# Shift and scale of the last four row steps on VectorE, two stages merged, and part of the weight splitting on GpSimd

## The chip, the cores and the metric

The kernel runs on one core of a Trainium2 chip. The metric is the device time of one execution, in microseconds (us); lower is better.

## The reference, cut to what matters

One layer of a diffusion trunk: a first feed-forward half step, a mixer (attention and spatial gating), a second feed-forward half step. Each is modulated by nine vectors that come out of one product with `w_ada`. 128 context and 256 latent tokens, D = 2048, float32.

```python
def adaln(cvec, w_ada, b_ada):
    m = jax.nn.silu(cvec) @ w_ada + b_ada
    return jnp.split(m, N_MOD, axis=-1)

def swiglu_sublayer(x, g, w_gate, w_up, w_down, shift, scale, gate):
    h = rms_norm(x, g) * (1 + scale) + shift
    f = (jax.nn.silu(h @ w_gate) * (h @ w_up)) @ w_down
    return x + 0.5 * gate * f
...
        x_ctx = swiglu_sublayer(x_ctx, ffn1_norm[l], ffn1_w_gate[l], ffn1_w_up[l], ffn1_w_down[l],
                                m_ctx[0], m_ctx[1], m_ctx[2])
```

The change concerns `m[0]` (shift) and `m[1]` (scale) of the first half step, which the first products need.

## The kernel before

All products run in three passes of matmuls: a weight piece is split into a rounded upper part `whi` (ScalarE, L250) and a lower part `wlo` (VectorE, L251), the activations into `hh` and `hl`; `three` (L282 to L284) multiplies lower by upper, upper by lower, upper by upper. Work goes in half steps of 24 matmuls, called slots here: `half()` hands out one split weight half, runs what was set for this slot with `later`, and counts the slot up; `ahead()` splits weights up to four halves ahead. Weights come in chunks of two halves through SyncE's queue into three raw buffers (`pump`, L200).

The first quarter of gate and up (six groups `g`, four PSUM banks each, `first_quarter_staged`) runs in stages over the 16 row steps `k` of D, so that it can begin before all of shift and scale is known: `BLOCKS` gives the steps of a stage. At the end of a stage VectorE adds each bank to a partial sum in SBUF (`part_gh`, `part_gl`, L724). The banks come from a pool of five (`acc`); from the slot of `switch` on, the fourth bank of a group comes from another pool (`mp`). Steps below the last stage are multiplied by unnormalised rows (`make_raw`, L502 and L507); for the last stage the rows are normalised (`make_h`: L527 on VectorE, L537 on ScalarE, L541 on VectorE), and the partial sums are scaled by GpSimd (L726) and shifted by ScalarE (L730).

Shift and scale come from chunks of `w_ada` that TensorE multiplies (`ada_chunk`, L345), one behind each of the first 28 slots, loaded by GpSimd's queue into two buffers (`rawa`). When a unit of steps is complete, `settle` runs `ada_unit`: selection matmuls (L364), bias (L369), scale (L388), then the rows. The other seven vectors are computed later on VectorE from transposed tiles: `ada_tile` (L436) multiplies a tile of `w_ada` with the broadcast vectors `csb`, silu already applied (L405), and sums along the row.

The squares for the norm run at slots 9, 12, 16 and 22 (ScalarE L447 and L452, VectorE L455), the norm at slot 24. Each engine runs its instructions in the order in which the program is written.

Of the kernel before, what the change touches and what calls it, by code (L numbers as in the profile page):

```python
# [35 lines left out]
G0 = QUARTERS[0]  # L36
SEGS = ((0, TC), (TC, T))
TS = T + 2
BLOCKS = ((0, 2), (2, 4), (4, 6), (6, 8), (8, 12), (12, 16))
NPE = 0  # L40
ADA_UNITS = tuple(((0, k0, k1), (1, k0, k1)) for k0, k1 in BLOCKS) + ((tuple((2, k, k + 4) for k in range(0, NPE, 4)),) if NPE else ())
ADA_AFTER = (1,) * (28 + NPE)
NSEL = 4


# [69 lines left out]
class Kernel:  # L115
# [4 lines left out]
    def setup(self):  # L120
        tc, nc, ctx, a = self.tc, self.nc, self.ctx, self.a
        self.main = ctx.enter_context(tc.tile_pool(name="main", bufs=1))
        self.rot = ctx.enter_context(tc.tile_pool(name="rot", bufs=2))
        self.wp = ctx.enter_context(tc.tile_pool(name="wp", bufs=NWP))
        self.acc = ctx.enter_context(tc.tile_pool(name="acc", bufs=5, space=bass.MemoryType.PSUM))
        self.mp = ctx.enter_context(tc.tile_pool(name="mp", bufs=3, space=bass.MemoryType.PSUM))
        self.dram = ctx.enter_context(tc.tile_pool(name="spill", bufs=1, space=bass.MemoryType.DRAM))

        self.par = self.tile1([P, NPAR], "par")
        self.ones = self.tile1([P, P], "ones")  # L130
        nc.vector.memset(self.ones, 1.0 / 1024.0)
# [17 lines left out]
        self.freed = {"W": 0, "A": 0}  # L149
        self.next_split = 0  # L150
# [32 lines left out]
    def pump(self):  # L183

        nc = self.nc
        room = {"W": self.room, "A": NADA}
        while True:
            can = [self.order[k][n] for k, n in self.issued.items()
                   if n < min(len(self.order[k]), self.freed[k] + room[k])]
            if not can:  # L190
                return
            c = min(can)
            k = self.kinds[c]
            if k == "A":
                raw = self.start.tile([P, CK * CW], F32, tag="rawa", name="rawa", bufs=NADA)
                src = self.a["wada_s"][self.issued[k]]
            else:
                raw = self.wp.tile([P, CK * CW], F32, tag="raw", name="raw", bufs=NRAW)
# [3 lines left out]
            self.issued[k] += 1  # L202

    def first_loads(self):

# [7 lines left out]
        for c in order:  # L213
            k = self.kinds[c]
            i = self.issued[k]
            if k == "A" and i < NADA:
                raw = self.start.tile([P, cols], F32, tag="rawa", name="rawa", bufs=NADA)
            else:
                raw = self.wp.tile([P, cols], F32, tag="raw", name="raw", bufs=NRAW)
# [17 lines left out]
        self.freed["W"] = NADA - na  # L237

    def ahead(self, n=NWP):

        nc = self.nc
        while len(self.split) < n and self.next_split < len(self.pieces):
            c, half = self.pieces[self.next_split]
            if half is not None:
                if c not in self.raw:
                    break
                src = self.raw[c][:, half * 1024:(half + 1) * 1024]
                hi = self.wp.tile([P, 1024], F32R, tag="whi", name="whi")
# [12 lines left out]

    def half(self):
# [131 lines left out]
    def csb_load(self, kh, slot):  # L394
# [309 lines left out]
    def first_quarter_staged(self):  # L704
# [38 lines left out]
        for st, (k0, k1) in enumerate(BLOCKS):  # L743
            for pairs in stage_halves(st):
# [4 lines left out]
                if slot == 0:  # L749
# [374 lines left out]
    def run(self):  # L1124
# [15 lines left out]
        with ExitStack() as st:  # L1140
# [30 lines left out]
            one = [(2, k) for k in range(NPE, KT)] + [(j, k) for j in (3, 4) for k in range(KT)]  # L1171
# [84 lines left out]
def layout(i):  # L1256
# [75 lines left out]
    for qt in range(2):  # L1332
        for kr in range(4):
# [38 lines left out]
```

## Time and profile before

| | |
|---|---|
| median of 3 runs | 2826.48 us (2826.29 to 2827.67) |
| the profiled execution, its own time | 2826.2 us |
| its span | 2824.1 us |
| TensorE matmuls busy | 2797.0 us, 99% |
| VectorE, ScalarE, GpSimd busy | 65%, 36%, 7% |
| DMA | 524.89 MB, mean 186 GB/s |

The span is what the profiler saw from first to last instruction; the time holds what lies around it as well. Shares are means over the span: the first 220 us, where shift and scale are made, differ from the rest.

### The profile page before, as it was taken

The page shows a single profiled execution, that of the slowest core. Times are in us where ns is not written, and L with a number is a line of the kernel's source. Part 1 is how long each engine was busy: PE and PEld are TensorE (multiplying, and loading weights), DVE is VectorE, ACT ScalarE, POOL GpSimd, SP SyncE. Part 2 cuts the span into 40 slices and gives each one's busy share as a digit, 9 for nine tenths or more (in the row PEclk, how much of TensorE's full clock was granted, in tenths as well). Part 3 has the DMA queues.
Part 4 walks back from the last instruction along what each step waited for, and adds up shares of the span by engine and source line. Part 5 has one row for each costly group of instructions (what it writes and reads, how often), then busy time and mean ns, then how long its engine had stood idle before and what let it go on. Part 6 is the DMA issues. An engine that isn't in the chain of part 4 may idle for free.

```text
span 2824.1 us, 39182 instructions
## 1 busy us (share of the span) xinstructions
PE 2797.0 (99%) x15984; PEld 2711.1 (96%) x15984; DVE 1841.8 (65%) x2887; ACT 1015.3 (36%) x1454; POOL 187.4 (7%) x302
## 2 busy tenths in 40 slices
PE   8999999999999999999999999999999999999997
PEld 6889999999999999988888999999999999999997
DVE  4767889798999798765566877554444543333335
ACT  3345432322322244543344445333333223322342
POOL 0031011011111010000000000000000000000000
PEclk9999999999999999999999999999999999999999
DMA  8854676666667675454333653444444433333432
GB/s 349 311 190 166 219 251 240 237 239 241 250 241 253 246 257 197 147 170 141 125 120 116 256 222 137 149 159 162 165 155 151 163 127 129 125 121 138 157 132 80
DMA packets 100035, 524.89 MB, mean 186 GB/s; under 512 B 11024, under 2 KB 18832, under 8 KB 55056
## 3 DMA queue, kind: packets, MB, share of 16 engines
q1 hardware_dynamic: 62224, 371.39, 36.0%
q0 software_dynamic: 37632, 151.01, 15.6%
q8 instruction: 125, 2.05, 0.3%
q14 instruction: 54, 0.44, 0.0%
HBM read 511.88 MB, written 10.49 MB: 185 GB/s over the span
## 4 chain that ended last, share of the span: by engine, by line
PE 99%; DVE 0%; DMA 0%; SPq 0%; ACT 0%; issue 0%; DVEq 0%
PE acc L282 24%; PE acc L284 24%; PE acc L283 24%; PE mp L282 7%; PE mp L284 7%; PE mp L283 6%; PE acc L307 2%; PE acc L308 2%; PE acc L309 2%; PE mp L345 1%; PE mp L858 0%; PE mp L908 0%; PE mp L938 0%; DMA raw<-wada_s 0%; DVE x L1240 0%; PE acc L756 0%
## 5 line engine op out<-in xcount | busy, mean ns | idle before, releaser
L251 DVE TENSOR_TENSOR wlo<-raw,whi 128x1024 fp32r<-128x1024 f32 x640 | 784.5, 1227 | 808.5 <-ACT whi L250 808.1
L250 ACT CAST whi<-raw 128x1024 fp32r<-128x1024 f32 x640 | 670.6, 1050 | 1425.0 <-PE mp L284 1149.9
L282 PE MATMUL acc<-hh,wlo 128*128 128x384 f32 (+1 forms) x2744 | 933.5, 340 | 0.0
L284 PE MATMUL acc<-hh,whi 128*128 128x384 f32 (+1 forms) x2744 | 927.6, 338 | 0.0
L283 PE MATMUL acc<-hl,whi 128*128 128x384 f32 (+1 forms) x2744 | 925.6, 337 | 0.0
L282 PEld LDWEIGHTS acc<-hh,wlo 128*128 128x128 f32 x2744 | 516.6, 188 | 25.5 <-issue 11.3
L283 PEld LDWEIGHTS acc<-hl,whi 128*128 128x128 f32 x2744 | 518.0, 189 | 0.8
L284 PEld LDWEIGHTS acc<-hh,whi 128*128 128x128 f32 x2744 | 516.6, 188 | 0.0
L282 PE MATMUL acc<-gh,wlo 128*128 128x384 f32 x1056 | 357.6, 339 | 0.0
L283 PE MATMUL acc<-gl,whi 128*128 128x384 f32 x1056 | 354.3, 336 | 0.0
L284 PE MATMUL acc<-gh,whi 128*128 128x384 f32 x1056 | 352.8, 334 | 0.0
L436 DVE CUSTOM_DVE_ANT_0 scr<-adaw,csb,par 128x1024 bf16<-128x1024 f32 x224 | 287.3, 1282 | 4.4
L436 DVE CUSTOM_DVE_ANT_0 scr<-adaw,csb,m 128x1024 bf16<-128x1024 f32 x224 | 287.3, 1282 | 4.2
L284 PE MATMUL mp<-hh,whi 128*128 128x384 f32 (+1 forms) x704 | 237.8, 338 | 0.0
L282 PE MATMUL mp<-hh,wlo 128*128 128x384 f32 (+1 forms) x704 | 237.2, 337 | 0.0
L283 PE MATMUL mp<-hl,whi 128*128 128x384 f32 (+1 forms) x704 | 237.0, 337 | 0.0
L421 POOL DMA_DIRECT2D adaw<-wada_t x224 | 118.5, 529 | 1447.9 <-DVE m L436 1352.8
L284 PEld LDWEIGHTS acc<-gh,whi 128*128 128x128 f32 x1056 | 198.5, 188 | 0.0
L283 PEld LDWEIGHTS acc<-gl,whi 128*128 128x128 f32 x1056 | 198.3, 188 | 0.0
L282 PEld LDWEIGHTS acc<-gh,wlo 128*128 128x128 f32 x1056 | 198.0, 188 | 0.0
L283 PEld LDWEIGHTS mp<-hl,whi 128*128 128x128 f32 x704 | 132.7, 189 | 0.0
L282 PEld LDWEIGHTS mp<-hh,wlo 128*128 128x128 f32 x704 | 132.5, 188 | 0.0
(170 smaller groups left out, 2238.5 us busy)
## 6 DMA issues: line engine op xcount, KB each, us to landing
raw<-ws SPq DMA_DIRECT2D x319, 1024.0 KB, 4.9
adaw<-wada_t POOLq DMA_DIRECT2D x224, 512.0 KB, 4.0
rawa<-wada_s POOLq DMA_DIRECT2D x26, 1024.0 KB, 5.9
csb<-crow POOLq DMA_DIRECT2D x6, 1024.0 KB, 7.9
keep<-x SPq DMA_DIRECT2D x8, 768.0 KB, 6.8
rawa<-wada_s SPq DMA_DIRECT2D x4, 1024.0 KB, 8.7
bias<-bias SPq DMA_DIRECT2D x16, 256.0 KB, 4.9
xo<-xT SPq DMA_DIRECT2D x16, 192.0 KB, 5.5
```

The source lines that it names most:

```text
L250: nc.scalar.copy(hi, src)
L251: nc.vector.tensor_sub(lo, src, hi.bitcast(F32))
L282: nc.tensor.matmul(o, lhsT=wl, rhs=xh, start=first, stop=False)
L283: nc.tensor.matmul(o, lhsT=wh, rhs=xl, start=False, stop=False)
L284: nc.tensor.matmul(o, lhsT=wh, rhs=xh, start=False, stop=last)
L307: nc.tensor.matmul(o, lhsT=xh, rhs=wl, start=first and kk == 0, stop=False)
L308: nc.tensor.matmul(o, lhsT=xl, rhs=wh, start=False, stop=False)
L309: nc.tensor.matmul(o, lhsT=xh, rhs=wh, start=False, stop=last and kk == 1)
L345: nc.tensor.matmul(self.ada_bank[r:r + 32, :cols], lhsT=self.csil[:, nsub * kc + q, w0:w0 + 32], rhs=raw[:, q * cols:(q + 1) * cols], star ...
L421: self.nc.gpsimd.dma_start(out=t, in_=self.a["wada_t"][j - 2, kt, kh])
L436: nc.vector.tensor_tensor_reduce(out=scr, in0=t, in1=self.csb[:, v, :], scale=1.0, scalar=init, op0=ALU.mult, op1=ALU.add, accum_out=acc)
```

## The change

Stages three and four (steps 4 to 6 and 6 to 8) become one; `w_ada` chunks on TensorE cover steps 0 to 11 only and end with slot 19. Steps 12 to 15 of shift and scale are made by `early()`: sixteen tiles of 128 x 1024 (two quantities, four steps, two halves of D), each reduced twice on VectorE (once for each vector) at the slots listed in `EARLY`. The vectors' halves are loaded at slots 8 and 19 into one of the three raw buffers, so weights have two until slot 34; their silu runs in four pieces on ScalarE in the two slots behind. From slot 8 to 33 lower parts of odd piece numbers are subtracted on GpSimd. `settle` runs in the middle of a slot too.

```diff
-BLOCKS = ((0, 2), (2, 4), (4, 6), (6, 8), (8, 12), (12, 16))
+BLOCKS = ((0, 2), (2, 4), (4, 8), (8, 12), (12, 16))
+UNITS = ((0, 2), (2, 4), (4, 6), (6, 8), (8, 12))
+EK = 12
-ADA_AFTER = (1,) * (28 + NPE)
+ADA_AFTER = (1,) * 20
+EARLY_CSB = (8, 19)
+EARLY = (11, 12, 13, 14, 15, 16, 17, 18, 22, 23, 24, 25, 26, 28, 30, 32)
+EARLY_END = 34
...
-                nc.vector.tensor_sub(lo, src, hi.bitcast(F32))
+                eng = nc.gpsimd if 8 <= self.slot < EARLY_END and self.next_split % 2 else nc.vector
+                eng.tensor_tensor(out=lo, in0=src, in1=hi.bitcast(F32), op=ALU.subtract)
...
+    def early(self):
...
+        def load(i):
+            if i < len(seq):
+                j, k, kh = seq[i]
+                nc.gpsimd.dma_start(out=tiles[i % 2], in_=self.a["wada_e"][j, k - EK, kh])
+
+        def vectors(kh):
+            if kh == 0:
+                self.ecsb = self.raw_buf("csb")
+                load(0)
+                load(1)
+            src = self.a["crow"]
+            nc.gpsimd.dma_start(out=self.ecsb.rearrange("p (a b) -> p a b", a=2),
...
+        def tile_of(i):
+            j, k, kh = seq[i]
+            for v in range(2):
...
+                nc.vector.tensor_tensor_reduce(out=scr, in0=tiles[i % 2], in1=self.ecsb[:, 1024 * v:1024 * (v + 1)],
+                                               scale=1.0, scalar=init, op0=ALU.mult, op1=ALU.add, accum_out=acc)
+            load(i + 2)
+
+        def end():
+            self.free.append(self.buf.pop("csb"))
+            self.room = NRAW
+            self.scales(0, C_G1, EK, KT)
+            self.make_h_later(self.rs, EK, EK + 1)
+            self.later(self.slot + 1, lambda: self.make_h(self.rs, EK + 2, EK + 3))
...
-                for kk, u in order:
+                for at, (kk, u) in enumerate(order):
+                    if at == 4:
+                        self.settle()
...
-            self.later(8, lambda: setattr(self, "room", NRAW))
+            self.early()
...
-            self.later(31 + NPE, switch)
+            self.later(36, switch)
...
-    nc = _bacc.Bacc("TRN2", target_bir_lowering=False, num_devices=1)
+    nc = _bacc.Bacc("TRN2", target_bir_lowering=False, num_devices=1, dynamic_dma_scratch_size=4096)
```

ScalarE around slots 9 and 10, before (casts L250, squares L452 and L447):

```order
L250 CAST whi<-raw 128x1024
L452 ACTIVATE ssq<-x 128x384
L447 ACTIVATE sq<-x 128x384 x3
L250 CAST whi<-raw 128x1024 x3
L447 ACTIVATE sq<-x 128x384 x4
```

and now (L262 is the cast, L456 the silu of the vectors, which lie in a `raw` buffer, L524 and L519 the squares):

```order
L262 CAST whi<-raw 128x1024
L456 ACTIVATE raw<-raw 128x512 x2
L524 ACTIVATE ssq<-x 128x384
L519 ACTIVATE sq<-x 128x384 x3
L262 CAST whi<-raw 128x1024
L456 ACTIVATE raw<-raw 128x512 x2
```

The silu pieces stand ahead of the squares of slot 9.

VectorE in slot 12, before (copy of a unit's result, subtraction, sums of squares, additions of the stage, then the unit's bias, scale and rows):

```order
L352 COPY adasb<-mp 128x256
L251 TENSOR_TENSOR wlo<-raw,whi 128x1024
L455 TENSOR_TENSOR ssq<-ssq,sq 128x384 x4
L724 TENSOR_TENSOR part_gh_223<-part_gh_223,acc 128x386
L724 TENSOR_TENSOR part_gl_225<-part_gl_225,acc 128x386
L724 TENSOR_TENSOR part_gh_227<-part_gh_227,acc 128x386
L724 TENSOR_TENSOR part_gl_229<-part_gl_229,acc 128x386
L369 TENSOR_TENSOR m_89<-mp,par 128x4
L369 TENSOR_TENSOR m_90<-mp,par 128x4
```

and now (L463 is the new reduction, L386 the bias, L405 the scale, L568 and L579 the rows' lower parts):

```order
L369 COPY adasb<-mp 128x256
L264 TENSOR_TENSOR wlo<-raw,whi 128x1024
L463 ISA escr,m_90<-eadaw,raw,par 128x1024
L463 ISA m_90 128x1
L463 ISA escr,m_90<-eadaw,raw,par 128x1024
L463 ISA m_90 128x1
L527 TENSOR_TENSOR ssq<-ssq,sq 128x384 x4
L386 TENSOR_TENSOR m_89<-mp,par 128x4
L386 TENSOR_TENSOR m_90<-mp,par 128x4
L405 SCALAR_TENSOR_TENSOR s<-m_90,par 128x4
L568 TENSOR_TENSOR hl<-m_89,hh 128x2x2
L579 SCALAR_TENSOR_TENSOR hl<-x,s,hh 128x128
```

The additions of this slot are gone; a tile's reductions stand ahead of the sums and of the unit.

VectorE in slot 35, before (one step of normalised rows, L527 and L541, then the additions):

```order
L527 SCALAR_TENSOR_TENSOR t<-x,s,rs 128x128
L527 SCALAR_TENSOR_TENSOR t<-x,s,rs 128x256
L541 SCALAR_TENSOR_TENSOR hl<-t,m_89,hh 128x128
L541 SCALAR_TENSOR_TENSOR hl<-t,m_89,hh 128x256
L724 TENSOR_TENSOR part_gh_486<-part_gh_486,acc 128x386
```

and now (the last of what stands there: four lower parts L613 of the first pair are ahead of these rows):

```order
L599 SCALAR_TENSOR_TENSOR t<-x,s,rs 128x128
L599 SCALAR_TENSOR_TENSOR t<-x,s,rs 128x256
L599 SCALAR_TENSOR_TENSOR t<-x,s,rs 128x128
L599 SCALAR_TENSOR_TENSOR t<-x,s,rs 128x256
L613 SCALAR_TENSOR_TENSOR hl<-t,m_89,hh 128x128
L613 SCALAR_TENSOR_TENSOR hl<-t,m_89,hh 128x256
L613 SCALAR_TENSOR_TENSOR hl<-t,m_89,hh 128x128
L613 SCALAR_TENSOR_TENSOR hl<-t,m_89,hh 128x256
L796 TENSOR_TENSOR part_gh_492<-part_gh_492,acc 128x386
```

Twelve operations on rows stand ahead of the first addition of slot 35, where there were four.

## Rows read from the trace of the kernel before

**Rows 1.** The page: part 1 (busy time) and part 4 (chain, by engine).

```profile
PE 2797.0 (99%) x15984; PEld 2711.1 (96%) x15984; DVE 1841.8 (65%) x2887; ACT 1015.3 (36%) x1454; POOL 187.4 (7%) x302
...
PE 99%; DVE 0%; DMA 0%; SPq 0%; ACT 0%; issue 0%; DVEq 0%
```

**Rows 2.** The chain in order of time: start us, us, what.

```profile
76.47 1.00 PE mp L345 x16
...
93.00 0.99 PE mp L345 x8
...
170.53 1.00 PE mp L345 x8
175.98 1.00 PE mp L345 x8
```

**Rows 3.** Timeline of ScalarE: start us, us, instruction, count, idle before and releaser.

```profile
181.51 1.05 ACT L250 CAST whi<-raw 128x1024 fp32r<-128x1024 f32 x1 [4.40 <-PE acc L284]
...
185.25 0.79 ACT L537 ACTIVATE hh<-t,m 128x128 fp32r<-128x128 f32 x2
...
190.92 1.05 ACT L250 CAST whi<-raw 128x1024 fp32r<-128x1024 f32 x1 [3.19 <-PE acc L284]
...
199.44 1.05 ACT L250 CAST whi<-raw 128x1024 fp32r<-128x1024 f32 x1 [1.30 <-issue]
```

**Rows 4.** Timeline of TensorE.

```profile
20.85 3.31 PE L756 MATMUL acc<-hh,whi 128*128 128x386 f32 x8 [1.35 <-ACT hh L502]
...
181.27 0.95 PE L364 MATMUL mp<-par,adasb 128*128 128x4 f32 x8
```

**Rows 5.** Timeline of GpSimd.

```profile
66.69 0.53 POOL L200 DMA_DIRECT2D rawa<-wada_s  x1 [4.85 <-PE mp L345]
...
188.07 1.01 POOL L726 TENSOR_TENSOR part_gl<-part_gl,rs 128x384 f32<-128x384 f32 x1
189.04 1.99 POOL L726 TENSOR_TENSOR part_gh<-part_gh,rs 128x384 f32<-128x384 f32 x1
```

**Rows 6.** Windows: stretch, busy us by engine, granted clock, DMA share, GB/s.

```profile
20.00:26.00 6.00, 5.06 (x19) 4.66 (x20) 2.88 (x6) 2.43 (x5) 0.00 (x0) 0.72 1.03 431
26.00:32.00 6.00, 6.00 (x45) 5.17 (x44) 4.84 (x6) 4.74 (x7) 0.67 (x1) 1.00 1.00 412
```

**Rows 7.** Tile csb: silu in ns (least, median, most), and landing.

```profile
L405 ACT ACTIVATE csb<-csb x6: 1912/1915/1919, 268.9 to 2051.4; 128x2048 f32<-128x2048 f32 x6
...
DMA to landing us min/median/max: 6.3/7.9/11.1
```

**Rows 8.** Timeline of ScalarE, slot 9.

```profile
74.05 0.52 ACT L452 ACTIVATE ssq<-x 128x384 f32<-128x384 f32 x1
```

**Rows 9.** Timeline of VectorE, slots 9 and 12.

```profile
77.12 0.55 DVE L724 TENSOR_TENSOR part_gh<-part_gh,acc 128x386 f32<-128x386 f32 x1
...
89.75 2.54 DVE L455 TENSOR_TENSOR ssq<-ssq,sq 128x384 f32<-128x384 f32 x4
...
94.07 0.22 DVE L369 TENSOR_TENSOR m<-mp,par 128x4 f32<-128x4 f32 x2
...
94.96 1.58 DVE L507 SCALAR_TENSOR_TENSOR hl<-x,s,hh 128x128 fp32r<-128x128 f32 x4 [0.31 <-ACT hh L502]
```

**Rows 10.** Timeline of VectorE: a tile of a later vector, and what follows.

```profile
274.55 1.28 DVE L436 CUSTOM_DVE_ANT_0 scr<-adaw,csb,par 128x1024 bf16<-128x1024 f32 x1
...
277.09 1.40 DVE L527 SCALAR_TENSOR_TENSOR t<-x,s,rs 128x128 f32<-128x128 f32 x4
```

**Rows 11.** Timeline of VectorE, slots 30 and 31.

```profile
188.33 1.83 DVE L251 TENSOR_TENSOR wlo<-raw,whi 128x1024 fp32r<-128x1024 f32 x1
...
192.01 1.23 DVE L251 TENSOR_TENSOR wlo<-raw,whi 128x1024 fp32r<-128x1024 f32 x1 [1.84 <-ACT whi L250]
193.15 0.74 DVE L527 SCALAR_TENSOR_TENSOR t<-x,s,rs 128x128 f32<-128x128 f32 x2
193.97 0.99 DVE L541 SCALAR_TENSOR_TENSOR hl<-t,m,hh 128x128 fp32r<-128x128 f32 x2
```

More of the change, by code (lines that the diff above doesn't have):

```diff
@@ L38 @@
 TS = T + 2
-BLOCKS = ((0, 2), (2, 4), (4, 6), (6, 8), (8, 12), (12, 16))
-NPE = 0
-ADA_UNITS = tuple(((0, k0, k1), (1, k0, k1)) for k0, k1 in BLOCKS) + ((tuple((2, k, k + 4) for k in range(0, NPE, 4)),) if NPE else ())
-ADA_AFTER = (1,) * (28 + NPE)
+BLOCKS = ((0, 2), (2, 4), (4, 8), (8, 12), (12, 16))
+UNITS = ((0, 2), (2, 4), (4, 6), (6, 8), (8, 12))
+EK = 12
+ADA_UNITS = tuple(((0, k0, k1), (1, k0, k1)) for k0, k1 in UNITS)
+ADA_AFTER = (1,) * 20
 NSEL = 4
@@ L149, in setup @@
         self.freed = {"W": 0, "A": 0}
+        self.free = deque(range(NRAW))
+        self.buf = {}
         self.next_split = 0
@@ L188, in pump @@
             can = [self.order[k][n] for k, n in self.issued.items()
-                   if n < min(len(self.order[k]), self.freed[k] + room[k])]
+                   if n < min(len(self.order[k]), self.freed[k] + room[k]) and (k == "A" or self.free)]
             if not can:
@@ L197, in pump @@
             else:
-                raw = self.wp.tile([P, CK * CW], F32, tag="raw", name="raw", bufs=NRAW)
+                raw = self.raw_buf(c)
                 src = self.a["ws"][self.issued[k]]
@@ L202, in pump, with raw_buf @@
             self.issued[k] += 1
+    def raw_buf(self, c):
+        i = self.free.popleft()
+        self.buf[c] = i
+        return self.wp.tile([P, CK * CW], F32, tag=f"raw{i}", name="raw", bufs=1)
     def first_loads(self):
@@ L218, in first_loads @@
             else:
-                raw = self.wp.tile([P, cols], F32, tag="raw", name="raw", bufs=NRAW)
+                raw = self.raw_buf(c)
             self.raw[c] = raw
@@ L258, in done @@
         del self.raw[c]
-        self.freed["W" if c in self.lent else self.kinds[c]] += 1
+        k = self.kinds[c]
+        if c in self.buf:
+            self.free.append(self.buf.pop(c))
+        if c not in self.lent:
+            self.freed[k] += 1
         self.pump()
@@ L408, in csb_load, with act @@
         self.later(slot + ACTD, act)
+    def early(self):
+        nc = self.nc
+        st = ExitStack()
+        pool = st.enter_context(self.tc.tile_pool(name="early", bufs=1))
+        tiles = [pool.tile([P, 1024], F32, tag=f"eadaw{i}", name="eadaw") for i in range(2)]
+        scr = pool.tile([P, 1024], BF16, tag="escr", name="escr")
+        self.early_pool = st
+        seq = [(j, k, kh) for kh in range(2) for k in range(EK, KT) for j in range(2)]
+        def load(i):
[9 more added lines that the diff above has]
+            nc.gpsimd.dma_start(out=self.ecsb.rearrange("p (a b) -> p a b", a=2),
+                                in_=bass.AP(tensor=src.tensor, offset=src.offset + kh * 1024,
+                                            ap=[[0, P], [D, 2], [1, 1024]]))
+        def act(q):
+            piece = self.ecsb[:, 512 * q:512 * (q + 1)]
+            nc.scalar.activation(piece, piece, AF.Silu)
+        def tile_of(i):
+            j, k, kh = seq[i]
+            for v in range(2):
+                acc = self.m[j][:, k, v:v + 1]
+                init = acc if kh else self.par[:, C_BADA + j * KT + k:C_BADA + j * KT + k + 1]
+                nc.vector.tensor_tensor_reduce(out=scr, in0=tiles[i % 2], in1=self.ecsb[:, 1024 * v:1024 * (v + 1)],
[7 more added lines that the diff above has]
+            self.later(self.slot + 1, lambda: self.make_h(self.rs, EK + 2, EK + 3))
+        for kh in range(2):
+            self.later(EARLY_CSB[kh], lambda kh=kh: vectors(kh))
+            for q in range(4):
+                self.later(EARLY_CSB[kh] + 1 + q // 2, lambda q=q: act(q))
+        for i, sl in enumerate(EARLY):
+            self.later(sl, lambda i=i: tile_of(i))
+        self.later(EARLY_END, end)
     def ada_queue(self, seq, more=False):
@@ L1170, in run @@
             self.later(24, norm)
-            one = [(2, k) for k in range(NPE, KT)] + [(j, k) for j in (3, 4) for k in range(KT)]
+            one = [(2, k) for k in range(KT)] + [(j, k) for j in (3, 4) for k in range(KT)]
             two = [(j, k) for j in (5, 6, 7) for k in range(KT)]
@@ L1178, in switch @@
                 assert not self.units
+                self.early_pool.close()
                 st0.close()
@@ L1284, in layout @@
     wada_s = np.concatenate(wada_s)
+    wada_e = wa[:, :2 * D].T.reshape(2, KT, P, 2, 1024)[:, EK:].transpose(0, 1, 3, 2, 4)
     wada_t = wa[:, 2 * D:].T.reshape(NMOD - 2, KT, P, 2, 1024).transpose(0, 1, 3, 2, 4)
@@ L1340, in layout @@
     wsT = f["w_s"][0].transpose(2, 0, 1)
-    arrs = dict(par=par, xT=xT, cT=cT, crow=crow, wada_s=wada_s, wada_t=wada_t, ws=ws, bias=bias,
+    arrs = dict(par=par, xT=xT, cT=cT, crow=crow, wada_s=wada_s, wada_t=wada_t, wada_e=wada_e, ws=ws, bias=bias,
                 ckT=ck, cv=cv, wsT=wsT, bs=f["b_s"][0])
```

1 line of the change is left out of this document (removed).

## The prediction, made before the result

> **What bounds the kernel now.** I read the page first: TensorE is busy 99% of the span and the chain that ended last is 99% PE [rows 1]. So time leaves the kernel only where TensorE gets fewer instructions, and enters it wherever TensorE has to wait. Next I read the chain in order of time for the shift-and-scale chunks (L345, one behind each of the first 28 half steps, called slots here). The chunks of slots 26 and 27 start 5.45 us apart [rows 2]. ScalarE casts one weight half per slot, released by TensorE; two slots without a chunk lie 8.52 us apart [rows 3], so a bare slot is 4.26 us, and a quarter of it (one PSUM bank, six matmuls) 1.07 us. A chunk costs 5.45 - 4.26 = 1.19 us.
>
> **What is removed.** Eight chunks (two quantities, four row steps each) leave TensorE: 8 x 1.19 = 9.5 us. The selection matmuls behind them go too, 0.95 us [rows 4]. Gain: **10.5 us**. VectorE also loses 24 additions of 0.55 us (one stage fewer), but it waits for TensorE there now, so alone they are worth nothing; they are spare time for what is added.
>
> **What is added, and why it doesn't stay hidden.** All of it goes on queues that run in order, in front of instructions for which TensorE waits. The rule to follow: five banks rotate, four in use, so the second bank of a slot comes free only when VectorE has made the first addition of the group before it. That addition is due 1.07 us after the next slot's start. An addition finished later stops TensorE.
>
> *(a) Slot 10: the first vectors.* The silu of the broadcast vectors stands on ScalarE in slot 9 ahead of the squares, whose sums stand on VectorE ahead of the additions of slot 9. It waits for the transfer. GpSimd issues that behind a chunk (issued at 66.69 [rows 5]) and two tiles, at about 68.3 (three issues of 0.53). In front of its end lie 1.05 MB of chunk, 1.05 MB of tiles, its own 1.05 MB and one weight chunk of 1.05 MB on the other queue: 4.2 MB. Two full queues moved 412 GB/s [rows 6], so 10.2 us, from about 2 us after 66.69 (an estimate: the first bytes are not seen alone): 78.9, and a little more, since its kind lands no sooner than 6.3 us after issue even on quiet queues [rows 7]. I take 79.5; bounds 74.6 (68.3 + 6.3) and 81. Then two silu pieces (a quarter of 1915 ns each [rows 7]: 0.96 us), and from the first square to the end of the first addition 77.67 - 74.05 = 3.62 us [rows 8, 9]. Slot 10 starts at 76.47 + 1.00 = 77.47 [rows 2], so the bank is due at 78.54. Wait: 79.5 + 0.96 + 3.62 - 78.54 = **5.6 us** (0.7 to 7).
>
> *(b) Slot 13: scaled rows of steps 6 and 7.* With stages three and four merged they are needed in slot 13, no longer in slot 18. The settling is pulled into the middle of slot 12, but on VectorE it stands behind the reduction of slot 12 and four sums of squares (2.54 us [rows 9]). A tile's two reductions take 277.09 - 274.55 = 2.54 us [rows 10]. Now the sums start at 89.75; slot 11's reduction makes its additions about 0.3 us late, so the shift addition (L369 of before) starts at 89.75 + 0.3 + 2.54 + 2.45 = 95.05. The lower parts end 96.54 - 94.07 = 2.47 us after it [rows 9]: 97.5. Slot 13 starts at 93.00 + 0.99 [rows 2] and its fifth matmul, due 0.7 us later at 94.7, needs the last of them: **2.8 us** (2 to 3.5).
>
> *(c) Slot 22: the second vectors.* Their load may start only when slot 18's reduction has read the first ones, about 1 us into slot 19; 6.3 to 11.1 us of landing [rows 7] put the silu, the eight scalings of steps 8 to 11 and the additions of slot 21 between in time and 3.6 us late. I take **0.5 us**, nearer the early end, because the last chunk load is over by then.
>
> *(d) Slots 24 and 26: VectorE full.* From the start of slot 22 to the first addition of slot 23 stand a rest of slot 21's additions (0.6 us if in time, 2.2 with the vectors late), a tile 2.54, four sums 2.54, a subtraction 1.2, a tile 2.54 and the addition 0.5: 11.5 us from 2.2. It is due 4.26 + 4.26 + 1.07 = 9.6 after that start: 1.9 us late (0.3 at best). Then three additions 1.4, a tile, three operations for the root 1.7, a subtraction, a tile, an addition: 9.9 us, against 3.2 + 4.26 + 1.07 = 8.5 of TensorE: 1.4 more. Together 3.3. To this comes the sharing with GpSimd. Before, a subtraction on VectorE that met a GpSimd multiplication took 1.83 us, where it takes 1.23 alone, and the next multiplication took 1.99, where it takes 1.01 [rows 5, 11]. The new GpSimd subtractions (1.01 x 1024/384 = 2.7 us, an estimate) meet reductions in slots 22 and 24: 0 to 2.7 us each; by the row's 0.61, 1.2 together. **4.5 us** (1.7 to 8.7).
>
> The Trainium skill ("SBUF — State Buffer", Who interferes with whom) says why: when VectorE has two SBUF inputs, it and GpSimd take a port pair for a whole instruction each, and the second is fully blocked. The rows agree (1.83 and 1.99 are each other's rest). By that rule each GpSimd subtraction can cost VectorE its full 2.7 us, more than the 1.2 us taken off it, and (d) would be 8.7; the sum above goes by the row.
>
> *(e) Slot 36: the last rows.* The four last steps are now made as two pairs in slots 34 and 35. In slot 35 ScalarE runs cast and eight shifts first, as it did in slot 29: 185.25 - 181.51 = 3.74 us, ending 3.9 into the slot [rows 3]. The first pair's four operations there take two times 0.79 [rows 3], to 5.5, and VectorE's last lower part (0.99 for two [rows 11]) ends at 6.0; the second pair begins only there, and one step took 193.15 to 194.96 [rows 11], 1.8 us, two 2.7: 8.7. Only then come the additions of slot 35, the first at 9.2, due at 4.26 + 1.07 = 5.3: **3.9 us** (3 to 4.5). The extra bank, which the last stages had from slot 31 on, now comes with slot 36.
>
> *Clock.* When TensorE waited at 19.5 to 20.85, the granted clock of the next stretch fell to 0.72 on average (the lower level, 1.2 GHz, for a while) [rows 6], and eight matmuls took 3.31 us [rows 4], not 8 x 0.178 = 1.4: 1.9 us lost. I count it once, behind (a): **1.9 us**; none to three times are possible.
>
> **Free edits.** The eight tile pairs' DMAs carry the same bytes as the eight chunks, 8.4 MB; the two vector loads add 2.1 MB. Sixteen tiles' issues of 0.53 us fit GpSimd, which is idle 93% of the span [rows 1]. The weight queue runs two deep instead of three until slot 34; casts stand four slots ahead of use, so a load may be 15 us late before TensorE sees it. What the smaller descriptor area costs no row shows; I take nothing, and if it holds issues back, loads come late as in the third rival.
>
> **Sum.** -10.5 + 5.6 + 2.8 + 0.5 + 4.5 + 3.9 + 1.9 = +8.7 us. The profiled execution took 2826.2 (span 2824.1 and 2.1 around it), 0.3 below the median shown: 2834.9, and with that 0.3 **2835**. A measurement of this kernel can tell about 0.2%, 5.6 us, from no change.
>
> **Rivals.** *First, not slower: the vectors land early.* Everything in (a) is one landing time. At 74.6 the wait is 0.7 us and the clock doesn't fall: -10.5 + 0.7 + 2.8 + 0.5 + 4.5 + 3.9 = +1.9, 2828. It decides below about 76.5, where the sum passes 5.6. For it: DMA engines were idle just ahead of 68 us. Against: four megabytes are then asked for at once. 0.26.
>
> *Second, faster: the banks have more slack than I count.* If TensorE doesn't wait for the first addition of the slot before, (a), (d), (e) shrink to under 1 us each and only (b) stays: -10.5 + 2.8 + 0.5 + 2 = -5 to -7, about 2820. For it: no such wait over 0.8 us is in the trace of before. Against: there the additions end within a microsecond of their due time (77.67 against 78.54 in slot 10), which leaves no room for 2.54 us. 0.16.
>
> *Third, worse: DMA full from slot 11 to 18.* Chunk 1.05, tile 0.52 and weights 0.52 MB in 5.45 us are 385 GB/s, with 0.79 MB of x twice on top, against 412 [rows 6]. If queues run less than full, chunks or tiles come late: some 4 us, 2839. 0.13.
>
> *Fourth, worse: the port rule in full,* (d) at 8.7: 2839. 0.15.
>
> The forecast itself, waits as summed, has 0.30. Slower by over 0.2%: forecast, third and fourth, 0.58. Within 0.2%: the first, 0.26. Faster: the second, 0.16. The range must reach into the second's and hold the dearer bounds of (a) and (d): 2821 to 2845; the likeliest case's own is 2830 to 2840.
>
> **What would show it.** L345 with eight chunks fewer; TensorE idle in slots 10, 13, 24, 26 and 36, with VectorE as releaser (the addition to the parts, or the lower part of the scaled rows); the vectors' landing near 79.5 us; GpSimd's subtractions over 2.7 us where they meet reductions; a granted clock under 1.00 after the first wait. The prediction is wrong if TensorE's idle time in the first 220 us stays under 5 us: then the second rival holds. It is wrong in its sizes if the waits lie elsewhere, above all on L345 for its chunks.

## The result and the profile after

The changed kernel took **2846.79 us** (median of 6 runs, 2845.0 to 2847.51) beside 2826.78 us of the kernel before (6 runs): ratio 1.0069, 95% interval 1.0058 to 1.0079. It is 20.0 us slower; 8.7 were forecast, and the time lies 1.8 us outside the range. The page answers to [rows 1]: parts 1 and 4.

```profile
PE 2798.6 (98%) x15912; PEld 2716.6 (96%) x15912; DVE 1875.6 (66%) x2916; ACT 1018.2 (36%) x1462; POOL 217.0 (8%) x320
...
PE 94%; DVE 3%; DMA 2%; ACT 1%; issue 1%; POOL 0%; SPq 0%; DVEq 0%; POOLq 0%; ACTq 0%
```

TensorE has 72 instructions fewer and is busy 1.6 us *more*: some of them ran slower. VectorE and DMA now stand in the chain that ended last. Next the waits of TensorE from 28 to 260 us (line waited at, releaser: us in total, times, longest) in the changed kernel:

```profile
PE acc L299 <- DVE part_gh L796: 15.5, 7, 4.4
PE acc L299 <- ACT hh L574: 2.1, 1, 2.1
PE mp L362 <- DMA rawa<-wada_s: 0.7, 1, 0.7
PE acc L299 <- ACT hh L609: 0.4, 1, 0.4
```

The same stretch as one window, in the changed kernel:

```profile
28.00:260.00 232.00, 212.95 (x1267) 190.40 (x1260) 177.39 (x276) 95.34 (x170) 73.48 (x72) 0.96 0.66 247
```

and the same window of the kernel before:

```profile
28.00:260.00 232.00, 232.00 (x1450) 205.99 (x1447) 159.57 (x271) 102.39 (x179) 44.00 (x54) 1.00 0.66 250
```

Before, TensorE never stopped here and had its full clock. After, it stands still for 232 - 212.95 = 19.1 us and has less than its full clock in part of the rest. Where the clock fell is read from shorter windows (columns as in [rows 6]), the three around slot 10 and then around slots 24, 32 and 36:

```profile
80.00:84.00 4.00, 0.12 (x1) 0.00 (x0) 1.67 (x4) 3.68 (x7) 0.00 (x0) 0.93 0.96 371
84.00:88.00 4.00, 3.48 (x11) 3.48 (x12) 3.94 (x8) 1.22 (x3) 0.00 (x0) 0.50 0.07 29
88.00:92.00 4.00, 4.00 (x28) 3.11 (x27) 1.46 (x3) 1.04 (x1) 0.13 (x1) 0.72 0.71 262
...
166.00:170.00 4.00, 1.92 (x8) 1.92 (x9) 3.96 (x9) 1.11 (x3) 2.12 (x2) 0.85 0.19 52
170.00:174.00 4.00, 4.00 (x19) 4.00 (x18) 3.86 (x6) 0.88 (x1) 1.27 (x2) 0.73 0.70 243
...
208.00:212.00 4.00, 3.04 (x11) 3.04 (x12) 4.00 (x7) 1.40 (x3) 3.02 (x3) 0.72 0.71 262
212.00:216.00 4.00, 4.00 (x21) 4.00 (x21) 2.86 (x5) 1.98 (x5) 4.00 (x3) 0.86 0.00 0
230.00:236.00 6.00, 4.56 (x14) 4.56 (x15) 4.51 (x8) 1.11 (x2) 4.54 (x4) 0.52 0.06 8
236.00:242.00 6.00, 6.00 (x33) 6.00 (x33) 2.16 (x3) 4.51 (x10) 2.63 (x5) 0.91 0.88 346
```

What a window lost is its length times (1 - clock): 3.4 us behind slot 10, 1.7 behind slot 24, 1.7 behind slot 32, 3.4 behind slot 36, together **10.2 us**. Full clock is 2.4 GHz, and 0.50 is 1.2 GHz throughout. Each drop stands behind a wait of TensorE. Waits 19.1 + clock 10.2 - gain 10.5 (the forecast's figure; tested in e5 and e11) = +18.8 us, against 20.0 measured.

The first wait, step by step (slot 10 of the changed kernel): a piece of the chain in order of time,

```profile
69.59 10.44 DMA raw<-crow
```

and timelines of ScalarE, VectorE and TensorE:

```profile
80.11 1.15 ACT L456 ACTIVATE raw<-raw 128x512 f32<-128x512 f32 x2 [6.46 <-DMA raw<-crow]
...
82.12 1.89 DVE L527 TENSOR_TENSOR ssq<-ssq,sq 128x384 f32<-128x384 f32 x3 [7.09 <-ACT sq L519]
83.92 0.55 DVE L796 TENSOR_TENSOR part_gh<-part_gh,acc 128x386 f32<-128x386 f32 x1
...
84.53 0.69 PE L299 MATMUL acc<-hh,wlo 128*128 128x386 f32 x1 [4.40 <-DVE part_gh L796]
```

Read it downwards: the vectors land at 80.0, ScalarE had waited 6.46 us for them with the squares behind it, VectorE 7.09 us for the squares with the additions behind it, TensorE 4.40 us for the first addition. In slot 13 the rows of steps 6 and 7 stand behind four sums of squares (timeline of VectorE, then TensorE):

```profile
101.20 2.54 DVE L527 TENSOR_TENSOR ssq<-ssq,sq 128x384 f32<-128x384 f32 x4
...
104.55 1.57 DVE L579 SCALAR_TENSOR_TENSOR hl<-x,s,hh 128x128 fp32r<-128x128 f32 x4 [0.31 <-ACT hh L574]
...
104.96 0.44 PE L299 MATMUL acc<-hh,wlo 128*128 128x386 f32 x1 [2.15 <-ACT hh L574]
```

And slot 28 waits, of which the prediction had nothing, for the additions of slot 27, behind the reductions of slot 26 (timelines of VectorE, then GpSimd):

```profile
180.41 6.44 DVE L463 CUSTOM_DVE_ANT_0 escr<-eadaw,raw,m 128x1024 bf16<-128x1024 f32 x1
...
186.89 1.29 DVE L463 CUSTOM_DVE_ANT_0 escr<-eadaw,raw,m 128x1024 bf16<-128x1024 f32 x1
...
180.45 1.00 POOL L798 TENSOR_TENSOR part_gl<-part_gl,rs 128x384 f32<-128x384 f32 x1
181.42 1.00 POOL L798 TENSOR_TENSOR part_gh<-part_gh,rs 128x384 f32<-128x384 f32 x1
182.39 1.01 POOL L798 TENSOR_TENSOR part_gl<-part_gl,rs 128x384 f32<-128x384 f32 x1
183.36 2.40 POOL L264 TENSOR_TENSOR wlo<-raw,whi 128x1024 fp32r<-128x1024 f32 x1
```

A reduction that takes 1.28 us elsewhere took 6.44: it ends 1.1 us after the last of four GpSimd instructions that ran one behind the other (183.36 + 2.40 = 185.8). TensorE waited 1.9 us for it.

### The profile page after: what moved, and what is told of

Read it like the earlier page. It is cut to its first block, busy times and chain, and to the rows that moved or that the text cites. A ratio compares the mean times of both kernels' runs of the same rounds, so it can differ in the third digit from the quotient of the medians.

```text
span 2844.6 us, 39103 instructions
## 1 busy us (share of the span) xinstructions
PE 2798.6 (98%) x15912; PEld 2716.6 (96%) x15912; DVE 1875.6 (66%) x2916; ACT 1018.2 (36%) x1462; POOL 217.0 (8%) x320
## 4 chain that ended last, share of the span: by engine, by line
PE 94%; DVE 3%; DMA 2%; ACT 1%; issue 1%; POOL 0%; SPq 0%; DVEq 0%; POOLq 0%; ACTq 0%
PE acc L299 23%; PE acc L301 22%; PE acc L300 22%; PE mp L299 6%; PE mp L301 6%; PE mp L300 6%; PE acc L324 2%; PE acc L325 2%; PE acc L326 2%; DVE escr L463 1%; DMA raw<-crow 1%; PE mp L932 0%; PE mp L362 0%; PE mp L982 0%; PE mp L1012 0%
## 5 line engine op out<-in xcount | busy, mean ns | idle before, releaser
L262 ACT CAST whi<-raw 128x1024 fp32r<-128x1024 f32 x640 | 670.3, 1050 | 1434.3 <-PE mp L301 1153.1
```

## The experiments

All times beside the kernel before on the same chip; "waits" and "clock" are TensorE's idle time and the time lost to the lower clock between 28 and 260 us, read as above. The account is waits + clock - gain, where the gain is 1.31 us (10.5 / 8) for each chunk that the kernel no longer has on TensorE.

| kernel | time less before, us | waits | clock | account |
|---|---|---|---|---|
| changed kernel | +20.0 | 19.1 | 10.2 | +18.8 |
| e1 lower parts on VectorE | +13.6 | 14.2 | 8.5 | +12.2 |
| e2 squares before silu | +13.4 | 14.2 | 10.2 | +13.9 |
| e3 merged stage alone | +1.3 | 0.3 | 0 | +0.3 |
| e4 descriptor area alone | 0.0 | 0 | 0 | 0 |
| e5 no early work | -4.9 | 3.7 | 3.4 | -3.4 |
| e6 three stalls | +0.7 | 0.9 | 0 | +0.9 |
| e7 spread | +4.2 | 11.9 | 0 | +1.4 |
| e8 spread, GpSimd | +11.4 | 15.6 | 3.4 | +8.6 |
| e9 half of it | -3.8 | 1.4 | 0 | -3.9 |
| e10 three longer stalls | +10.6 | 7.2 | 3.4 | +10.6 |
| e11 no early work, rows later | -5.6 | 3.3 | 0 | -7.2 |
| e12 products on VectorE | +4.4 | 11.2 | 3.4 | +4.1 |

The account misses the time by up to 1.6 us, and by 2.8 in e7 and e8; it comes from one profiled execution of each. It also leaves out the first 28 us, where none of the new work runs yet: the profiled executions of e7 and e8 lost 6.8 us to the lower clock there, the kernel before 1.7, and the chunk that starts at 27.07 us in the kernel before starts at 28.55 and 28.63 in theirs. That is 1.5 of the 2.8 us, and it is not the change's.

**e1: no GpSimd subtractions.**

```diff
-                eng = nc.gpsimd if 8 <= self.slot < EARLY_END and self.next_split % 2 else nc.vector
-                eng.tensor_tensor(out=lo, in0=src, in1=hi.bitcast(F32), op=ALU.subtract)
+                nc.vector.tensor_sub(lo, src, hi.bitcast(F32))
```

> The changed kernel with every lower part on VectorE again; nothing else differs. Theory (waits plus the clock that falls behind them): the reductions of slots 22 to 30 take 1.28 us each again (one took 6.44 us beside GpSimd), the waits behind slots 28 and 32 (1.9 and 1.8 us) and the drop of the clock behind each late one (3.4 us at the lower level, 1.7 us lost) go, the one at slot 24 stays, since VectorE gets 1.2 us of subtraction per second slot: 5 to 7 us less than the changed kernel, 2840 to 2842. Rival one (the port sharing is the whole excess over the forecast): 10 to 12 us less, 2835. Rival two (VectorE is simply full and needs GpSimd's help): the waits at slots 24 to 28 grow by 1.2 us each and draw more clock drops: 2847 to 2853.

Measured 2840.6 us, ratio 1.0048 (1.0036 to 1.0061): 6.2 less than the changed kernel, the time of the theory. The waits in slots 28 and 32 are 0.8 and 0 us, as it had them. Two others changed as well: the wait of slot 22 (1.8 us) is gone, and one of 2.1 us for a chunk of `w_ada` is new at 143.7 us, with 1.7 us of clock lost behind it; whether the edit made these is not shown. GpSimd's subtractions cost more than they give, but they are a third of the excess, not all of it.

**e2: squares ahead of the silu in slot 9.**

```diff
+            self.later(9, lambda: squares(0))
             self.early()
...
-            for k, sl in ((0, 9), (4, 12), (8, 16), (12, 22)):
+            for k, sl in ((4, 12), (8, 16), (12, 22)):
```

> The changed kernel with one order changed: in slot 9 ScalarE does the four squares before the two silu pieces of the broadcast vectors, so that VectorE's sums and additions no longer stand behind the vectors' landing. Theory (a wait costs itself and the clock behind it): the wait of 4.4 us in slot 10 goes and with it the 6.8 us at the lower clock (3.4 us lost): 7.8 us less, 2839. Rival (the clock would have fallen at another place anyway, or the lost clock is nothing): 4.4 us less, 2842.4. If the landing wasn't the cause: no change, 2846.8.

Measured 2840.44 us, ratio 1.0047 (1.0034 to 1.006): 6.4 less, between theory and rival. The wait of slot 10 is gone, so its cause is shown. But its clock drop is not saved: it now stands behind slot 13, whose wait has grown to 3.05 us (TensorE's timeline of e2, and under it the window there):

```profile
97.46 0.69 PE L299 MATMUL acc<-hh,wlo 128*128 128x386 f32 x1 [3.05 <-ACT hh L574]
```

```profile
92.00:110.00 18.00, 14.95 (x72) 12.29 (x71) 15.29 (x30) 4.71 (x9) 2.28 (x5) 0.81 0.84 311
```

**e3 and e4: single parts on the kernel before.**

```diff
-BLOCKS = ((0, 2), (2, 4), (4, 6), (6, 8), (8, 12), (12, 16))
+BLOCKS = ((0, 2), (2, 4), (4, 8), (8, 12), (12, 16))
+UNITS = ((0, 2), (2, 4), (4, 6), (6, 8), (8, 12), (12, 16))
...
+                    if at == 4:
+                        self.settle()
```

> The kernel before with one part of the change: stages three and four as one of four k tiles, with the settling in the middle of the half step; all 28 chunks on TensorE, no reductions on VectorE. Theory (slot 13's wait comes from the rows of steps 6 and 7, of which the reduction of slot 12 carries 2.5 us): without the reduction the rows end 2.5 us earlier, and the wait of 2.15 us in slot 13 is gone or under 0.5 us: 2826 to 2828. Rival (merging alone makes the rows late, by the sums of squares of slot 12): 2 to 3 us of wait, with a clock drop 4 to 6: 2829 to 2833.

```diff
-    nc = _bacc.Bacc("TRN2", target_bir_lowering=False, num_devices=1)
+    nc = _bacc.Bacc("TRN2", target_bir_lowering=False, num_devices=1, dynamic_dma_scratch_size=4096)
```

> The kernel before with the smaller descriptor area alone. Theory: no transfer waits for it, 2826 to 2828, the profile as before. Rival (it holds issues on GpSimd's queue back): chunks and tiles land later and the time is 2830 or more.

e3: 2828.31 us, ratio 1.0004 (0.9995 to 1.0013); its only wait from 28 to 260 us is 0.3 us, none of it in slot 13. e4: 2827.04 us, ratio 1.0 (0.9991 to 1.0008). Both cost nothing that can be measured, so merging alone does not make the wait of slot 13. That the reduction in front of the rows makes it is seen from e2 and e9 below: both have the squares in slot 12, but e9 has no reduction there, and the wait is 0.4 us instead of 3.05, less by the 2.5 us of a tile.

**e5 and e11: without the new work on VectorE**, so the chunks' worth is seen. e11 differs from e5 in the last rows:

```diff
-            self.later(self.slot + 1, lambda: self.make_h(self.rs, EK + 2, EK + 3))
+            self.later(self.slot + 1, lambda: self.make_h_later(self.rs, EK + 2, EK + 3))
```

> The changed kernel with the new work on VectorE left out: no vectors, no tiles, no reductions, shift and scale of the last row block set to zero (so the last four k tiles are scaled with other numbers than the reference's); all lower parts on VectorE. It shows what the eight chunks are worth by themselves. Theory: the gain of 10.5 us is real, and nothing but the making of the last rows in slots 34 and 35 may still hold TensorE up (0 to 2.9 us of wait and 0 to 3.4 us of clock): 2816.5 to 2822. Rival (the chunks were worth less than 10.5 us, so that the waits alone explain the slower time): 2822 to 2827.

> The kernel of e5_no_early_work (the new work on VectorE left out, last four k tiles scaled with other numbers) with the second pair of the last rows made half step by half step in slots 35 and 36 instead of all in 35. Theory (the 2.5 us wait at slot 36 and the 6.8 us of lower clock behind it are the making of the last rows): both go, 4 to 6 us less than e5: 2816.5 to 2819. Rival (the wait only moves to slot 37, where the second pair is needed): 2821 to 2823.

e5: 2822.51 us, ratio 0.9983 (0.9974 to 0.9992). e11: 2821.59, 0.9979 (0.9971 to 0.9988). Adding their waits and clock back, the chunks are worth 4.9 + 3.7 + 3.4 = 12.0 and 5.63 + 3.33 = 9.0 us, on both sides of 10.5. The profiled executions themselves took 2823.48 and 2820.52 us, 1.0 above and 1.1 below their medians; with these times it is 11.0 and 10.0 us. In e5 the wait of 2.5 us at slot 36 stands without any reduction, so it is the making of the last rows. e11 came out at the rival's time: the wait split (1.2 us at slot 36, 1.7 at slot 37) instead of going, and though no clock fell in its profile, the time differs from e5's by less than the runs can tell.

**e6 and e10: does a wait alone bring the clock down?** Idle work on the VectorE of the kernel before (e10 has `range(14)`):

```diff
+            def stall():
+                t = self.tmp("t")
+                for _ in range(7):
+                    nc.vector.tensor_add(t, self.x[0], self.x[1])
+            for sl in (14, 20, 26):
+                self.later(sl, stall)
```

> The kernel before with three stalls added and nothing else: in slots 14, 20 and 26 VectorE makes seven additions of 384 elements that nobody reads, about 3.7 us, ahead of the additions to the parts. TensorE should wait some 2.8 us each time, 8.4 us together. Theory (the clock falls behind a wait and that costs as much again): each wait is followed by 3.4 us or 6.8 us at the lower clock, 1.7 or 3.4 us lost each: 2840 to 2846. Rival (the clock drops have to do with what the changed kernel does on other engines, or with its transfers, not with the waits): the clock stays at 1.00 and the time is 2835.

> The kernel before with the three idle stalls of VectorE twice as long: fourteen additions, 7.7 us, in slots 14, 20 and 26 (seven gave waits of 0, 0 and 0.9 us). TensorE should wait about 3, 3 and 4.7 us, 10.7 together. Theory (the clock falls behind a wait of that length and costs 1.7 or 3.4 us more each time): 5 to 10 us beyond the waits, 2842 to 2848. Rival (the drops have to do with other work in the changed kernel): the waits alone, clock 1.00, 2837 to 2839.

e6: 2828.15 us, ratio 1.0003 (0.9994 to 1.0012). Only one wait came of it, 0.9 us: VectorE had more room than I gave it, and the run says nothing about the clock. e10: 2837.85 us, ratio 1.0038 (1.0026 to 1.0051). Windows of e10 around its first two waits, 3.7 and 3.1 us:

```profile
107.00:112.00 5.00, 1.27 (x5) 0.94 (x5) 4.80 (x10) 0.00 (x0) 0.00 (x0) 0.93 0.77 297
112.00:116.00 4.00, 4.00 (x18) 3.75 (x17) 3.04 (x5) 0.00 (x0) 0.00 (x0) 0.66 0.00 0
146.00:150.00 4.00, 0.86 (x4) 0.62 (x3) 3.86 (x8) 0.00 (x0) 0.00 (x0) 0.85 0.94 360
150.00:154.00 4.00, 4.00 (x18) 3.77 (x16) 3.61 (x13) 3.10 (x10) 0.00 (x0) 0.72 0.07 29
```

The clock falls behind both, in a kernel without vectors, tiles or GpSimd subtractions: it is the waits. It cost 1.7 us behind each, and 7.2 + 3.4 is the 10.6 us measured (the third wait is 0.4 us, without a drop). e6, with half of the idle work and 0.9 us of wait, has no drop.

**e7, e8 and e12: the same sixteen tiles at better places.** e7 has e1's and e2's edits and

```diff
-EARLY_CSB = (8, 19)
-EARLY = (11, 12, 13, 14, 15, 16, 17, 18, 22, 23, 24, 25, 26, 28, 30, 32)
+EARLY_CSB = (8, 20)
+EARLY_SILU = (9, 22)
+EARLY = (11, 13, 14, 15, 16, 17, 18, 19, 24, 25, 26, 28, 29, 30, 32, 33)
...
-            for k, sl in ((0, 9), (4, 12), (8, 16), (12, 22)):
+            for k, sl in ((4, 14), (8, 18), (12, 22)):
```

with the last rows as in e11; e8 keeps the GpSimd subtractions; e12 is e7 with

```diff
-                    nc.gpsimd.tensor_tensor(out=part[:, :T], in0=part[:, :T], in1=self.rs, op=ALU.mult)
+                    nc.vector.tensor_mul(part[:, :T], part[:, :T], self.rs)
```

> The changed kernel with the same work at other places: all lower parts on VectorE; squares ahead of the silu in slot 9; no reduction in slot 12 and the second squares in slot 14, the third in 18; second vectors loaded in slot 20 and their silu in slots 22 and 23; later reductions in three slots of four; the second pair of the last rows made in slots 35 and 36. By the sums of its instructions VectorE then ends each slot's additions at or before their due time. Theory (all of the excess is waits for VectorE and the clock behind them, and they are a matter of places): no wait over 0.5 us, 2816 to 2819. Rival (VectorE has not the room for sixteen tiles of 2.54 us there, wherever they stand): waits of 5 us or more and clock drops, 2826 to 2835.

> The kernel of e7_spread with every second lower part on GpSimd again, as in the changed kernel. Theory (a GpSimd subtraction of 2.4 us takes as much from a reduction beside it as VectorE saves): reductions of 1.9 to 3.3 us and more in the slots with GpSimd, waits of 2 to 6 us with clock drops: 2819 to 2826, slower than e7. Rival (GpSimd's help is worth its price): the same as e7 or up to 2 us less.

> The kernel of e7_spread with the products of the parts on VectorE instead of GpSimd, so that GpSimd computes nothing there. Theory (GpSimd's products of 1.0 us hold VectorE's instructions with two SBUF inputs up, 4.08 us for a subtraction of 1.22): every subtraction takes 1.22 us and every reduction 1.28 us again; but 24 products of 0.55 us are added, about what the sharing cost, so the waits of slots 26 to 36 stay within 3 us of e7's: 2828 to 2833. Rival (long subtractions come from somewhere else): they stay at 1.8 to 4.1 us and the time is 2838 or more.

e7: 2831.64 us, ratio 1.0012 (1.0003 to 1.0021). e8: 2838.8, 1.004 (1.0027 to 1.0052). e12: 2831.63, 1.0015 (1.0006 to 1.0024). My theory for e7 fell: 11.9 us of waits stay, 10.2 of them from 170 us on. Groups of VectorE from 150 to 240 us (count, busy us, mean ns), first e7:

```profile
L264 DVE TENSOR_TENSOR wlo<-raw,whi 128x1024 fp32r<-128x1024 f32 x18 | 30.2, 1676 | 3.8 <-ACT whi L263 3.8
L463 DVE CUSTOM_DVE_ANT_0 escr<-eadaw,raw,m 128x1024 bf16<-128x1024 f32 x16 | 23.3, 1454 | 0.3
```

then e12:

```profile
L264 DVE TENSOR_TENSOR wlo<-raw,whi 128x1024 fp32r<-128x1024 f32 x17 | 20.7, 1220 | 2.5 <-ACT whi L263 2.5
L463 DVE CUSTOM_DVE_ANT_0 escr<-eadaw,raw,m 128x1024 bf16<-128x1024 f32 x16 | 20.5, 1281 | 0.3
L798 DVE TENSOR_TENSOR part_gh<-part_gh,rs 128x384 f32<-128x384 f32 x12 | 6.7, 558 | 0.4
```

and e8:

```profile
L464 DVE CUSTOM_DVE_ANT_0 escr<-eadaw,raw,m 128x1024 bf16<-128x1024 f32 x16 | 37.2, 2327 | 2.4 <-DMA eadaw<-wada_e 2.0
L265 DVE TENSOR_TENSOR wlo<-raw,whi 128x1024 fp32r<-128x1024 f32 x12 | 17.5, 1456 | 1.7 <-ACT whi L263 1.7
```

With GpSimd computing nothing both instructions take their bare time, which shows that GpSimd was what lengthened them. In e7 the products cost VectorE (1676 - 1220) x 18 + (1454 - 1281) x 16 ns = 11.0 us on these two groups and 2.2 on the last rows (L613 599 against 413 ns, L599 498 against 414, eight each); doing them itself costs 24 x 0.558 = 13.4 us: the same, and so is the time. In e8 the subtractions moved away save 30.2 - 17.5 = 12.7 us and the reductions grow by 37.2 - 23.3 = 13.9. VectorE needs per two slots four additions (2.2 us), two subtractions (2.4) and what the four products cost, 2.2 if it makes them: 6.8 of the 8.5 us that TensorE takes. Tiles of 2.54 us at three in four slots add 3.8, 10.6 in all: from slot 24 on, where e7 has eight of them, they don't fit.

**e9: half of it**, by that reading: only steps 14 and 15 on VectorE, no tile after slot 24, the last rows made as before; also e1's and e2's edits.

```diff
-UNITS = ((0, 2), (2, 4), (4, 6), (6, 8), (8, 12))
-EK = 12
-ADA_AFTER = (1,) * 20
+UNITS = ((0, 2), (2, 4), (4, 6), (6, 8), (8, 12), (12, 14))
+EK = 14
+ADA_AFTER = (1,) * 24
...
-EARLY_CSB = (8, 19)
-EARLY = (11, 12, 13, 14, 15, 16, 17, 18, 22, 23, 24, 25, 26, 28, 30, 32)
-EARLY_END = 34
+EARLY_CSB = (8, 16)
+EARLY_SILU = (9, 18)
+EARLY = (11, 13, 14, 15, 19, 21, 22, 24)
+EARLY_END = 26
...
-            self.later(36, switch)
+            self.later(31, switch)
```

> Half of the change: shift and scale of k tiles 14 and 15 alone on VectorE (eight tiles instead of sixteen, all in slots 11 to 24), those of 12 and 13 in four more chunks on TensorE behind slots 20 to 23; the merged stage kept; all lower parts on VectorE; the four last rows one by one in slots 28, 30, 32 and 34 and the extra banks from slot 31, as in the kernel before. Theory (VectorE has room for about eight tiles before GpSimd's products begin in slot 26, and none behind): no wait over 1 us and no clock drop behind one; gain 4 x 1.19 + 0.3 = 5.1 us: 2821.5 to 2824. Rival (eight tiles draw waits and clock drops too): 2826 to 2832.

Measured 2823.46 us (11 runs), ratio **0.9987** (0.9978 to 0.9996): faster than both kernels, by 3.8 us over the one before, as worked out. Its windows:

```profile
28.00:140.00 112.00, 110.57 (x754) 91.46 (x750) 79.07 (x138) 43.49 (x73) 15.87 (x29) 1.00 0.94 355
140.00:260.00 120.00, 120.00 (x717) 116.36 (x716) 94.99 (x146) 64.36 (x116) 33.44 (x31) 1.00 0.47 169
```

**Second profiles** of four kernels, unchanged (e13 the changed one, e14 the one before, e15 that of e7, e16 that of e10).

> The changed kernel a second time, for a second profile. Theory (the clock behind the waits is a property of the kernel and the main term that the forecast had too small): 7 to 12 us of clock lost between 28 and 260 us again (10.2 in the first profile), waits of 18 to 20 us at the same slots. Rival (the drops of the first profile were that execution's): under 4 us lost, and a span shorter by the difference, 2838.

> The kernel before a second time, for a second profile. Theory: no clock under 1.00 between 28 us and the last stage, since TensorE doesn't wait there; the stretch at the lower level between 15 and 28 us is longer or shorter by chance (3.4 in its first profile, 3.4 to 12.6 in others of kernels that are the same up to there). Rival: drops appear in 28 to 260 us without a wait.

> The kernel of e7_spread a second time. Its first profile shows waits of 2.5 us twice and 11.9 us together, and no drop behind them. Theory (whether a wait of 2 to 3 us draws a drop is not fixed by the wait): 0 to two stretches of 3.4 us this time. Rival (fixed by the kernel): none again.

> The kernel of e10_three_longer_stalls a second time. Theory (waits over 3 us draw a drop each time): behind both waits, 3.7 and 3.1 us, a stretch of 3.4 or 6.8 us at the lower level again. Rival (chance): one or none.

One run each: 2848.79, 2827.99, 2831.87 and 2838.08 us. e13's waits, and under them its window:

```profile
PE acc L299 <- DVE part_gh L796: 13.6, 6, 3.4
PE acc L299 <- ACT hh L574: 2.1, 1, 2.1
```

```profile
28.00:260.00 232.00, 215.05 (x1266) 192.39 (x1265) 176.65 (x274) 96.08 (x171) 73.48 (x72) 0.94 0.66 245
```

Waits 16.9 and 13.6 us of clock: an account of +20.0. So the drops belong to the kernel; which wait draws which drop does not. Behind slot 10 it lost 1.7 us this time instead of 3.4, behind slot 13 1.7 instead of nothing. Waits and clock can stand in for each other: behind slot 22 e13 lost 3.4 us of clock and has no wait in slot 24, where the first profile shows no drop and then a wait of 2.4 us. e14 shows no lower clock from 28 to 260 us. e15 waits 2.5 and 1.9 us where e7 had its two longest waits (2.5 each) and loses 1.7 us behind each; the first profile shows 1.00 there. e16 repeats e10's two drops. Of the eleven waits over 3 us in these profiles, ten have a drop behind them (not one of 3.45 us in e8, clock 1.00). Of those from 1.8 to 2.8 us some have one and some have none, and one drop of 1.7 us in e8 (clock 0.50 from 140 to 143 us) stands behind two short waits, of 0.54 and 0.67 us. What decides is open.

## Why the prediction was wrong

The direction and its reason were right: the gain is there (e5, e11) and waits of TensorE for VectorE outweigh it. The size was not, by 11.3 us.

- **The step that failed is Clock**: "I count it once, behind (a): 1.9 us; none to three times are possible." The first profile shows four drops and 10.2 us, the second six and 13.6. e10 shows that waits alone do it. The term was counted for one wait where the forecast's own list had four of 2.8 us and more, (a), (b), (d) and (e); at the price of the one row that it had, four come to 7.6 us. That price was not fixed either: a drop behind 28 us cost 1.7 or 3.4 us, and the stretch from which the row was read lost nothing in e10 and 6.8 us in e7, e8 and e13. Nor does every wait draw one (e7).
- **Gain 10.5**: 9.0 to 12.0 in e11 and e5, 10.0 and 11.0 by the profiled executions' own times. Right.
- **(a) 5.6**: 4.4 and 3.4 us in the two profiles, the mechanism shown by e2. Landing 80.0, forecast 79.5. The wait is shorter than forecast mainly because slot 10 began later: the chunk in front of it starts at 77.81 us, in the kernel before at 76.47.
- **(b) 2.8**: 2.15 us in both profiles, 3.05 in e2, where slot 10 holds nothing back; e3 shows that it needs more than the merged stage, and e9 beside e2 that it is the reduction.
- **(c) 0.5**: 1.8 and 3.2 us, half way to the late bound of 3.6 and near it. The early end, which the forecast took, was wrong: the second vectors landed 9.6 us after their issue (139.55 to 149.1).
- **(d) 4.5**: 2.4 + 0.8 us in slots 24 and 26, but 1.9 and 1.8 more in slots 28 and 32, 6.9 in all; in the second profile, where slot 24 has no wait, 4.6. Two things were missed: the reductions also meet GpSimd's products, and they wait for a whole run of GpSimd instructions (1.28 to 6.44 us), not 0.61 us as in [rows 11]. In the first profile the fourth rival (8.7) was nearer than the sum, in the second the sum. The Trainium skill ("SBUF — State Buffer", Who interferes with whom) says that a VectorE instruction with two SBUF inputs contends with GpSimd, and that the one who comes second is fully blocked. e12's return to 1.28 us agrees; the 6.44 us agree with the blocking, but here it lasted through four GpSimd instructions.
- **(e) 3.9**: 2.9 us (0.4 and 2.5), and in e5 the same without any reduction.
- **Free edits**: the descriptor area cost nothing (e4). "A load may be 15 us late" did not hold in slot 32, where ScalarE stood for a weight load (its timeline in the changed kernel, then VectorE's):

```profile
204.64 1.05 ACT L262 CAST whi<-raw 128x1024 fp32r<-128x1024 f32 x1 [5.95 <-DMA raw<-ws]
...
205.72 2.72 DVE L264 TENSOR_TENSOR wlo<-raw,whi 128x1024 fp32r<-128x1024 f32 x1 [3.53 <-ACT whi L262]
...
208.36 0.54 DVE L796 TENSOR_TENSOR part_gh<-part_gh,acc 128x386 f32<-128x386 f32 x1
```

  The load was late not for the matmuls that use it but for the queue: the subtraction stands on VectorE ahead of the additions. Two buffers alone don't make it late: e1, e7 and e12 have two as well, without GpSimd's subtractions, and ScalarE doesn't wait for a load there. Nor do the subtractions with two buffers always (e8 has no such wait); what makes this load late is not shown.
- **Rivals**: the first fell with the landing, the second with 19 us of waits; the third was not seen (no wait from 110 to 150 us in the changed kernel; e1, e7 and e12 have waits of 0.7 to 2.1 us for chunks there). The DMA engines that the first calls idle ahead of 68 us were busy 0.21 to 0.50 of the time from 66 to 69 us.

The waits forecast sum to 17.3 us and measured 19.1 in the first profile. That the sums lie so close is partly luck: (a), (b) and (e) came out 2.9 us shorter, (c) and (d) 3.7 longer, and about 1.0 is short waits that the forecast had not, 0.7 of it for a chunk at 44 us. In all, of the 11.3 us missing, 8.3 are the clock, 1.8 the waits, and 1.2 the account doesn't place.

## What to carry to other kernels

Where one engine is busy 99% of the time, price each stop of it with the clock that follows, not once but per stop: here 10.2 to 13.6 us of clock for 17 to 19 us of waits, and 0 to 3.4 us for 10 to 12 us of them in e7, its repetition and e12. An engine that is "65% busy" can be full in the one stage where the work is put; add up its instructions per step there, with what it loses to an engine it shares with. And an instruction that waits for data in an in-order queue is paid by what stands behind it: order it behind what is due first (e2), and take only as much as the stage holds (e9).

## What was not expected of the hardware

GpSimd's help to VectorE was worth nothing here in either form: 24 products moved off VectorE save 13.4 us and cost 13.2 in longer instructions beside them (e12 and e7), and subtractions moved off it saved 12.7 and cost 13.9 (e8). A VectorE instruction can wait for several GpSimd instructions in a row: 4.08 us for a subtraction of 1.22 behind three products in e7, 6.44 for a reduction of 1.28 in the changed kernel. The same kernel draws clock drops at different waits in different executions, while its time stays within 0.2%.
